# Delta rule block inverses: a second, transposed table in DRAM in place of on-chip transposes

## The chip, the cores and the metric

One Trainium2 chip (trn2), one core. The metric is the device time of one execution in microseconds (us). The kernel before takes 1786.38 us, the median of three runs (1785.5 to 1786.52).

## What is computed

The reference is one inference step of a hybrid decoder layer for 1024 prompt tokens and 8 sampled tokens. The part that the change touches is the gated delta rule of the prompt tokens, four heads of width 128. Cut to what matters:

```python
k = ...; beta = ...; g = cumsum(log decay)          # per head, per chunk
a_mat = where(strict, einsum('cd,sd->cs', k * beta, k) * decay, 0)
sol   = triangular_solve(eye + a_mat, rhs, lower=True)
# scan over chunks: v_new = u - w S;  o = q S + qk v_new;  S = S * decay + k^T v_new
```

The kernel does not solve the triangular system. It forms the inverse of the unit triangular matrix of each chunk of 128 tokens and each head and multiplies by it.

## The kernel before

The program is a single stream for five engines, written with a tile framework that plans the order of the instructions on each engine by a simulated timeline, and fills waits of one part with instructions of others. So the order on an engine is not the order in the code: projections, the top-k search, the query/key normalisation and the scan of the delta rule are interleaved. Within an engine the order is fixed once planned, and an instruction that waits holds up everything behind it on that engine. All DMAs of this part are issued by SyncE (SP), whose queue is in order too.

The parts around the change, in the order of the code:

- `w2`: for each of four heads, projections (`u_tile`), and `dl_local`, which stores the triangular matrices' 32 by 32 diagonal blocks into the DRAM table `d_b` and the whole blocks into `d_Bt`.
- `block_inverse`: loads all 128 diagonal blocks (4 block positions, 8 chunks, 4 heads), one block in each partition, 1024 numbers long, as `B`; inverts them at once by 31 steps of two VectorE instructions (L678 and L680) into `U`; stores `U` to the DRAM table `d_u` (L681). `B` and `U` are two of the four buffers of the tag "c", which `u_tile` uses too.
- `scan`: `dl_setup` clears `Ub` and `Bo` (two buffers each) and then `dl_chunk` runs for eight chunks. It loads six tiles (L1132), calls `dl_inverse`, and makes the chunk's output and the state for the next chunk.
- `dl_inverse(n)`: loads the four diagonal blocks of each head into `Ub` (L1089, four DMAs of 16 KB each), off-diagonal parts into `Bo` (L1092) and `Btl` (L1094); transposes `Ub` for the four heads on TensorE (L1097) into PSUM, tag `pi` with two buffers; copies that to `T0` on ScalarE (L1099); multiplies `Bo` by `T0` (L1102), copies the product to `P1` (L1104), multiplies by `Ub` (L1107) and subtracts (L1109). A second, smaller level follows (L1112 to L1123).
- The projections that fill the waits are the matmuls L163 to L165 with ScalarE evacuating their PSUM banks (L862 for the gates, L692 for queries and keys; two banks); the top-k search counts on ScalarE (L765) and VectorE (L768) in turn; `load_kv` (L993 to L1003) loads keys into the single buffer `kvn`, four small DMAs a round, and transposes them.

What shows as tile `T` in a row of the profile is `T0` or `T1`, since buffer numbers are left out there.

Of the kernel before, what the change touches and what calls it, by code (L numbers as in the profile page):

```python
# [9 lines left out]
F32 = mybir.dt.float32  # L10
# [4 lines left out]
AF = mybir.ActivationFunctionType  # L15
# [39 lines left out]
class K:  # L55
# [368 lines left out]
    def dram(self):  # L424
        dp = self.dp
        self.d_g = dp.tile([16, 128, T], F32, name="d_g")
        self.d_z = dp.tile([4, 128, T], F32, name="d_z")
        self.d_qT = dp.tile([4, 128, 1024], F32, name="d_qT")
        self.d_kT = dp.tile([4, 128, 1024], F32, name="d_kT")
        self.d_kn = dp.tile([1024, 512], F32, name="d_kn")  # L430
        self.d_vn = dp.tile([1024, 512], F32, name="d_vn")
        self.d_qk = dp.tile([128, 8, 4, 128], F32, name="d_qk")
        self.d_D = dp.tile([128, 8, 4, 128], F32, name="d_D")
        self.d_G = dp.tile([32, 128], F32, name="d_G")
        self.d_Bt = dp.tile([128, 8, 4, 128], F32, name="d_Bt")
        self.d_b = dp.tile([4, 8, 4, 32, 32], F32, name="d_b")
        self.d_u = dp.tile([4, 8, 4, 32, 32], F32, name="d_u")
        self.d_q = dp.tile([T, 512], F32, name="d_q")
        self.d_k = dp.tile([T, 128], F32, name="d_k")
        self.d_v = dp.tile([T, 128], F32, name="d_v")  # L440
        self.d_s = dp.tile([8, 6, 128], F32, name="d_s")
        self.d_y = dp.tile([8, 128, T], F32, name="d_y")
        self.d_ob = dp.tile([4, 128, T], F32, name="d_ob")
        self.d_x2 = dp.tile([8, 128, T], F32, name="d_x2")
        self.d_act = dp.tile([22, 128, T], F32, name="d_act")
        self.d_oa = dp.tile([8, 64, 1024], F32, name="d_oa")
# [218 lines left out]
    def block_inverse(self):  # L665

        nc, wk = self.nc, self.wk
        B = wk.tile([128, T], F32, name="c", tag="c", bufs=4)[:, 0:1024].rearrange("p (i c) -> p i c", c=32)
        U = wk.tile([128, T], F32, name="c", tag="c", bufs=4)[:, 0:1024].rearrange("p (i c) -> p i c", c=32)
        nc.sync.dma_start(B.rearrange("p i c -> p (i c)"), self.d_b.rearrange("b n h i c -> (b n h) (i c)"))  # L670
        nc.gpsimd.memset(U, 1.0)
        nc.gpsimd.affine_select(U, U, pattern=[[-1, 32], [1, 32]], compare_op=ALU.is_equal, fill=0.0, base=0,
                                channel_multiplier=0)
        t = self.scratch[:, 1600:1856]
        for j in range(31, 0, -1):
            w = 32 - j
            tv = t[:, :j * w].rearrange("p (a b) -> p a b", a=j)
            nc.vector.tensor_tensor(tv, B[:, 0:j, j:j + 1].to_broadcast([128, j, w]),  # L678
                                    U[:, j:j + 1, j:32].to_broadcast([128, j, w]), op=ALU.mult)
            nc.vector.tensor_tensor(U[:, 0:j, j:32], U[:, 0:j, j:32], tv, op=ALU.subtract)  # L680
        nc.sync.dma_start(self.d_u.rearrange("b n h i c -> (b n h) (i c)"), U.rearrange("p i c -> p (i c)"))  # L681

    def qkv(self, m):

# [384 lines left out]
    def dl_setup(self):  # L1069
        nc, wk, cp = self.nc, self.wk, self.cp  # L1070
        self.dn = cp.tile([128, 1], F32, name="dn")
        nc.sync.dma_start(self.dn, self.I['delta_norm'].rearrange("a c -> c a"))
        self.Ub, self.Bo = [], []
        for j in range(2):
            u = self.up.tile([128, 4, 128], F32, name=f"Ub{j}", bufs=1)
            b = self.up.tile([128, 4, 128], F32, name=f"Bo{j}", bufs=1)
            nc.gpsimd.memset(u, 0.0)
            nc.gpsimd.memset(b, 0.0)
            self.Ub.append(u)
            self.Bo.append(b)  # L1080
        self.St = None

    def dl_inverse(self, n):

        nc, wk = self.nc, self.wk
        Ub, Bo = self.Ub[n % 2], self.Bo[n % 2]
        for b in range(4):
            s = slice(32 * b, 32 * b + 32)
            nc.sync.dma_start(Ub[s, :, s], self.d_u[b, n].rearrange("h i c -> i h c"))  # L1089
        for b in (0, 2):  # L1090
            s, d = slice(32 * b, 32 * b + 32), slice(32 * b + 32, 32 * b + 64)
            nc.sync.dma_start(Bo[s, :, d], self.d_Bt[s, n, :, d])  # L1092
        Bt = wk.tile([64, 4, 64], F32, name="Btl", tag="Btl", bufs=1)
        nc.sync.dma_start(Bt, self.d_Bt[0:64, n, :, 64:128])  # L1094
        p = self.pd("pi")
        for h in range(4):
            nc.tensor.transpose(p[:, h], Ub[:, h], self.ident)  # L1097
        T0 = wk.tile([128, 4, 128], F32, name="T0", tag="T0", bufs=1)
        nc.scalar.activation(T0, p, AF.Copy)  # L1099
        p = self.pd("pi")  # L1100
        for h in range(4):
            nc.tensor.matmul(p[:, h], Bo[:, h], T0[:, h], start=True, stop=True)  # L1102
        P1 = wk.tile([128, 4, 128], F32, name="P1", tag="P1", bufs=1)
        nc.scalar.activation(P1, p, AF.Copy)  # L1104
        p = self.pd("pi")
        for h in range(4):
            nc.tensor.matmul(p[:, h], P1[:, h], Ub[:, h], start=True, stop=True)  # L1107
        U = wk.tile([128, 4, 128], F32, name="U1", tag="U1", bufs=2)
        nc.vector.tensor_tensor(U, Ub, p, op=ALU.subtract)  # L1109
        p = self.pd("pi")  # L1110
        for h in range(4):
            nc.tensor.transpose(p[:64, h, 0:64], U[0:64, h, 0:64], self.ident[:64, :64])  # L1112
        T1 = wk.tile([64, 4, 64], F32, name="T1", tag="T1", bufs=1)
        nc.scalar.activation(T1, p[:64, :, 0:64], AF.Copy)
        p = self.pd("pi")
        for h in range(4):
            nc.tensor.matmul(p[:64, h, 0:64], Bt[:, h, :], T1[:, h], start=True, stop=True)
        P2 = wk.tile([128, 4, 64], F32, name="P2", tag="P2", bufs=1)
        nc.vector.tensor_copy(P2[64:128], p[:64, :, 0:64])
        p = self.pd("pi")  # L1120
        for h in range(4):
            nc.tensor.matmul(p[:64, h, 0:64], P2[64:128, h], U[64:128, h, 64:128], start=True, stop=True)
        nc.scalar.activation(U[0:64, :, 64:128], p[:64, :, 0:64], AF.Copy, scale=-1.0)  # L1123
        return U
# [711 lines left out]
```

## Time and profile before

| | us |
|---|---|
| median of three runs | 1786.38 |
| the profiled execution | 1784.55 |
| its span, first to last instruction | 1782.70 |
| TensorE (PE) busy | 1736.5 |
| VectorE (DVE) busy | 1207.6 |
| ScalarE (ACT) busy | 852.3 |
| GpSimd (POOL) busy | 42.6 |

The profiled execution lies 1.83 us (0.1%) under the median; 1.85 us of it lie outside the span. Times in rows are microseconds from the span's start. Starts and durations of matmuls overlap their neighbours, because they are pipelined; what one costs in a run is the distance of its end from the end before it.

### The profile page before, as it was taken

Reading aid. Unit: us, or ns where it says so; the run is one execution under the profiler, and the core shown is the slowest. Engines: PE = TensorE matmul, PEld = TensorE weight load, DVE = VectorE, ACT = ScalarE, POOL = GpSimd, SP = SyncE. Lnnn points to the kernel's source line nnn. Section 1 sums busy time; section 2 is a strip of 40 time slices with the busy share of each in tenths; the row PEclk is TensorE's granted clock in tenths of the full one; section 3 lists DMA queues with packets and bytes.
Section 4 is the critical chain, followed back from the end, with each engine's and each line's share of the span. In section 5 each row is a group of like instructions: output and inputs, shape, how many; then the busy total and the mean of one; then the engine's idle time right before and its main releaser. Section 6 shows DMA issues by size and latency. Waiting matters only on the chain.

```text
span 1782.7 us, 31712 instructions
## 1 busy us (share of the span) xinstructions
PE 1736.5 (97%) x12276; PEld 1662.9 (93%) x12276; DVE 1207.6 (68%) x2776; ACT 852.3 (48%) x1575; POOL 42.6 (2%) x68
## 2 busy tenths in 40 slices
PE   5999999999999999999999999999999999999999
PEld 5998989999999988878889999999999999999998
DVE  7775658999898867797757488776666665734222
ACT  4568467777834436587634244443333333412012
POOL 3001100000000000010000000000000000000000
PEclk9999999999999999999999999999999999999999
DMA  6114434433645542254568444332222223722122
GB/s 196 40 34 143 138 106 138 145 92 116 176 128 156 170 143 89 84 190 138 173 215 265 135 133 144 96 115 82 84 72 82 85 78 121 229 85 80 46 80 69
DMA packets 293594, 218.00 MB, mean 122 GB/s; under 512 B 39292, under 2 KB 267456, under 8 KB 292412
## 3 DMA queue, kind: packets, MB, share of 16 engines
q1 hardware_dynamic: 291716, 205.50, 38.1%
q0 software_dynamic: 1728, 10.49, 1.7%
q8 instruction: 96, 1.57, 0.4%
q14 instruction: 54, 0.44, 0.1%
HBM read 154.17 MB, written 61.87 MB: 121 GB/s over the span
## 4 chain that ended last, share of the span: by engine, by line
PE 84%; DMA 5%; DVE 5%; issue 3%; ACT 2%; SPq 0%; POOL 0%; ACTq 0%; DVEq 0%; POOLq 0%
PE pj L163 15%; PE pj L165 15%; PE pj L164 15%; PE F L1708 2%; PE F L1710 2%; PE F L1709 2%; PE A L1708 2%; PE A L1709 2%; PE A L1710 2%; PE D L1708 2%; PE D L1710 2%; PE D L1709 2%; PE PT L1055 1%; PE B L1709 1%; PE B L1708 1%
## 5 line engine op out<-in xcount | busy, mean ns | idle before, releaser
L163 PE MATMUL pj<-xhi,whi 128*128 128x344 f32 x912 | 298.6, 327 | 5.3 <-ACT gs L862 4.3
L165 PE MATMUL pj<-xhi,wlo 128*128 128x344 f32 x912 | 295.4, 324 | 0.0
L164 PE MATMUL pj<-xlo,whi 128*128 128x344 f32 x912 | 294.2, 323 | 0.0
L187 ACT ACTIVATE whi<-wraw 128x1024 fp32r<-128x1024 f32 (+4 forms) x126 | 115.3, 915 | 249.3 <-PE pj L164 208.7
L163 PEld LDWEIGHTS pj<-xhi,whi 128*128 128x128 f32 x912 | 172.8, 189 | 9.4 <-ACT gs L862 5.8
L164 PEld LDWEIGHTS pj<-xlo,whi 128*128 128x128 f32 x912 | 172.8, 189 | 2.0 <-issue 1.1
L165 PEld LDWEIGHTS pj<-xhi,wlo 128*128 128x128 f32 x912 | 172.7, 189 | 1.5
L164 PE MATMUL pj<-act,whi 128*128 128x344 f32 x528 | 170.2, 322 | 0.0
L163 PE MATMUL pj<-act,whi 128*128 128x344 f32 x528 | 169.8, 322 | 0.0
L165 PE MATMUL pj<-act,wlo 128*128 128x344 f32 x528 | 168.8, 320 | 0.3 <-DVE wlo L188 0.3
L188 DVE TENSOR_TENSOR wlo<-wraw,whi 128x1024 fp32r<-128x1024 f32 (+3 forms) x104 | 116.4, 1119 | 48.8 <-ACT whi L187 46.7
L1772 DVE TENSOR_TENSOR x<-pj,x 128x344 f32<-128x344 f32 x96 | 48.6, 514 | 141.6 <-PE pj L165 141.4
L768 DVE TENSOR_SCALAR_CACHE_REDUCE kvb<-S,cand 128x384 bf16<-128x384 f32 (+3 forms) x128 | 103.7, 810 | 2.0
L165 PEld LDWEIGHTS pj<-act,wlo 128*128 128x128 f32 x528 | 99.3, 188 | 0.5 <-DVE wlo L188 0.5
L163 PEld LDWEIGHTS pj<-act,whi 128*128 128x128 f32 x528 | 99.3, 188 | 0.5
L164 PEld LDWEIGHTS pj<-act,whi 128*128 128x128 f32 x528 | 99.3, 188 | 0.0
L1709 PE MATMUL A<-hb,wlo 128*128 128x258 f32 x328 | 92.6, 283 | 0.0
L1708 PE MATMUL A<-hb,wlo 128*128 128x258 f32 x328 | 92.5, 282 | 0.0
L1710 PE MATMUL A<-hb,wlo 128*128 128x258 f32 x328 | 92.3, 282 | 0.0
L1708 PE MATMUL D<-hb,wx 128*128 128x258 f32 x308 | 87.1, 283 | 0.0
L1709 PE MATMUL D<-hb,wx 128*128 128x258 f32 x308 | 87.0, 282 | 0.0
L1710 PE MATMUL D<-hb,wx 128*128 128x258 f32 x308 | 87.0, 283 | 0.0
(595 smaller groups left out, 4803.0 us busy)
## 6 DMA issues: line engine op xcount, KB each, us to landing
wraw<-in_w_gate_up SPq DMA_DIRECT2D x50, 512.0 KB
wraw<-in_w_in SPq DMA_DIRECT2D x38, 512.0 KB
d_act<-x SPq DMA_DIRECT2D x41, 258.0 KB
araw<-d_act SPq DMA_DIRECT2D x20, 516.0 KB
d_g<-gs SPq DMA_DIRECT2D x48, 172.0 KB
wraw<-in_w_out SPq DMA_DIRECT2D x16, 512.0 KB
wraw<-in_w_branch SPq DMA_DIRECT2D x12, 512.0 KB
wraw<-in_w_down SPq DMA_DIRECT2D x16, 384.0 KB
```

The costliest lines, as they stand in the source:

```text
L163: nc.tensor.matmul(ps, lh, rh, start=(j == 0), stop=False)
L164: nc.tensor.matmul(ps, lh, rl, start=False, stop=False)
L165: nc.tensor.matmul(ps, ll, rh, start=False, stop=(j == last))
L187: self.nc.scalar.activation(hi, src, AF.Copy)
L188: self.nc.vector.tensor_tensor(lo, src, hi.bitcast(F32), op=ALU.subtract)
L768: nc.vector.tensor_scalar(junk[:r, :n], s, thr[:r, j:j + 1], 0.0, op0=ALU.is_lt, op1=ALU.add, accum_out=cnt[:r, j:j + 1])
L1055: nc.tensor.transpose(p[:, j, :], P[j][:, 128 * s:128 * s + 128], self.ident)
L1708: nc.tensor.matmul(p, lh, rh, start=(first and k == 0), stop=False, skip_group_check=True)
L1709: nc.tensor.matmul(p, lh, rl, start=False, stop=False, skip_group_check=True)
L1710: nc.tensor.matmul(p, ll, rh, start=False, stop=(k == 3), skip_group_check=True)
L1772: nc.vector.tensor_tensor(xv, p, xv, op=ALU.add)
```

## The change

`block_inverse` writes the inverted blocks a second time: a ScalarE copy (Copy activation) reads `U` with rows and columns of each block exchanged and writes over `B`, which is then stored to a new DRAM table `d_ut`. `dl_inverse` no longer transposes: it loads `T0` from `d_ut` by four DMAs a chunk, ahead of those of `Ub`. `T0` has one buffer for all eight chunks, and its off-diagonal parts are cleared once in `dl_setup`. Eight times four transposes and eight ScalarE copies go; one ScalarE copy, one store of 512 KB, 32 loads of 16 KB and one clearing come.

```diff
         self.d_b = dp.tile([4, 8, 4, 32, 32], F32, name="d_b")
+        self.d_ut = dp.tile([4, 8, 4, 32, 32], F32, name="d_ut")
         self.d_u = dp.tile([4, 8, 4, 32, 32], F32, name="d_u")
...
         nc.sync.dma_start(self.d_u.rearrange("b n h i c -> (b n h) (i c)"), U.rearrange("p i c -> p (i c)"))
+        nc.scalar.activation(B, U.rearrange("p i c -> p c i"), AF.Copy)
+        nc.sync.dma_start(self.d_ut.rearrange("b n h i c -> (b n h) (i c)"), B.rearrange("p i c -> p (i c)"))
...
+        self.T0 = self.up.tile([128, 4, 128], F32, name="T0", bufs=1)
+        nc.gpsimd.memset(self.T0, 0.0)
         self.St = None
...
-        Ub, Bo = self.Ub[n % 2], self.Bo[n % 2]
+        Ub, Bo, T0 = self.Ub[n % 2], self.Bo[n % 2], self.T0
         for b in range(4):
             s = slice(32 * b, 32 * b + 32)
+            nc.sync.dma_start(T0[s, :, s], self.d_ut[b, n].rearrange("h i c -> i h c"))
             nc.sync.dma_start(Ub[s, :, s], self.d_u[b, n].rearrange("h i c -> i h c"))
...
-        p = self.pd("pi")
-        for h in range(4):
-            nc.tensor.transpose(p[:, h], Ub[:, h], self.ident)
-        T0 = wk.tile([128, 4, 128], F32, name="T0", tag="T0", bufs=1)
-        nc.scalar.activation(T0, p, AF.Copy)
         p = self.pd("pi")
         for h in range(4):
             nc.tensor.matmul(p[:, h], Bo[:, h], T0[:, h], start=True, stop=True)
```

## Rows read from the trace of the kernel before

**Rows 1.** The page: busy time of each engine; chain that ended last, by engine.
```profile
PE 1736.5 (97%) x12276; PEld 1662.9 (93%) x12276; DVE 1207.6 (68%) x2776; ACT 852.3 (48%) x1575; POOL 42.6 (2%) x68
...
PE 84%; DMA 5%; DVE 5%; issue 3%; ACT 2%; SPq 0%; POOL 0%; ACTq 0%; DVEq 0%; POOLq 0%
```

**Rows 2.** Stages around the change: stretch, length, busy time, PEclk, DMA share, GB/s.
```profile
345.00:440.00 95.00, 95.00 (x631) 94.82 (x630) 88.25 (x256) 72.91 (x127) 2.62 (x7) 1.00 0.38 110
440.00:560.00 120.00, 117.46 (x836) 113.01 (x836) 109.19 (x289) 70.52 (x156) 0.00 (x0) 0.99 0.53 151
560.00:640.00 80.00, 76.18 (x575) 71.14 (x575) 62.50 (x206) 36.11 (x92) 0.00 (x0) 0.98 0.55 155
```

**Rows 3.** Groups by line, 440 to 640: busy us, mean ns, idle before.
```profile
L1097 PE MATMUL pi<-ident,Ub 128*128 128x128 f32 x32 | 5.2, 285 | 0.0
...
L1099 ACT ACTIVATE T<-pi 128x512 f32<-128x512 f32 x8 | 4.7, 591 | 1.1 <-PE pi L1097 1.1
```

**Rows 4.** Timeline of PE, chunk 0: start, duration, instruction.
```profile
451.95 0.32 PE L165 MATMUL pj<-xhi,wlo 128*128 128x344 f32 x1
452.11 0.60 PE L1097 MATMUL pi<-ident,Ub 128*128 128x128 f32 x4
452.46 0.40 PE L163 MATMUL pj<-xhi,whi 128*128 128x344 f32 x1
```

**Rows 5.** Chain in order of time: start, what it adds to the chain, what.
```profile
445.38 5.40 DMA zs<-d_z
...
469.66 0.35 PE pj L165
...
474.86 0.59 PE pi L1097 x4
...
479.77 0.89 PE pi L1102 x8
```

**Rows 6.** ScalarE's instructions of 1024 and of 512 columns, by shape and by line.
```profile
L187 ACT ACTIVATE whi<-wraw 128x1024 fp32r<-128x1024 f32 x72 | 76.1, 1057 | 94.1 <-PE pj L164 71.6 <-issue 9.5 <-PE F L164 5.4
...
L1288 ACT ACTIVATE Ss<-tp x2: 1019/1021/1023, 246.3 to 248.1; 8x512 f32<-8x512 f32 x2
```

**Rows 7.** Timeline of DVE: the last step of the block inverses.
```profile
439.59 0.18 DVE L680 TENSOR_TENSOR c<-c,kvb 128x31 f32<-128x31 f32 x1
```

**Rows 8.** Timeline of ACT just after it.
```profile
439.58 1.03 ACT L765 ACTIVATE kvb<-S,cand 128x896 bf16<-128x896 f32 x1
...
442.42 0.77 ACT L862 ACTIVATE gs<-pj 128x344 f32<-128x344 f32 x2
```

**Rows 9.** Timeline of PE at two stalls; in brackets idle time and its releaser.
```profile
440.79 0.27 PE L701 MATMUL tq<-ident,st 128*8 128x128 f32 x1
442.90 0.43 PE L163 MATMUL pj<-xhi,whi 128*128 128x344 f32 x1 [1.84 <-ACT gs L862]
...
565.93 0.41 PE L997 MATMUL tq<-ident,kvn 128*128 128x128 f32 x2 [0.30 <-DMA kvn<-d_k]
```

**Rows 10.** Stretches: busy times, granted clock, DMA share, GB/s.
```profile
443.60:447.10 3.50, 3.50 (x15) 3.50 (x14) 2.77 (x14) 2.76 (x5) 0.00 (x0) 0.51 0.84 232
...
445.00:450.00 5.00, 5.00 (x27) 5.00 (x27) 4.67 (x14) 3.72 (x9) 0.00 (x0) 0.79 0.91 270
...
455.00:460.00 5.00, 4.30 (x32) 4.11 (x31) 3.97 (x10) 4.61 (x13) 0.00 (x0) 1.00 1.01 306
```

**Rows 11.** Timeline of SP's DMA issues: start, time on the queue, DMA, count.
```profile
439.80 0.34 SPq L681 DMA_DIRECT2D d_u<-c  x1
...
445.82 1.98 SPq L1089 DMA_DIRECT2D Ub<-d_u  x4
...
480.70 1.00 SPq L1092 DMA_DIRECT2D Bo<-d_Bt  x2
...
560.80 3.35 SPq L993 DMA_DIRECT2D kvn<-d_k  x4
```

**Rows 12.** The matmuls that read T0: min/median/max ns, first and last start.
```profile
L1102 PE MATMUL pi<-T,Bo x64: 272/275/421, 456.3 to 613.1; 128*128 128x128 f32 x64
```

## The prediction

> **What bounds the kernel now.** I read the page first: TensorE is busy for 97% of the span and makes up 84% of the chain that ended last [rows 1]. Then the stages that the change touches, by stretches: while the block inverses run on VectorE (up to 440) TensorE has no idle time at all, in the first part of the scan (440 to 560) it lacks 2.5 us, in the second (560 to 640) 3.8 us [rows 2]. So no chain of the delta rule sets the time; TensorE's own work does, plus a few stalls. The scan's waits are filled with projections that have to be done anyway. What the change saves counts as far as it is TensorE time or one of those stalls; a shorter latency of a chunk's inverse counts for nothing. What it adds on ScalarE, SP or the DMA engines counts only where TensorE already waits for these.
>
> **What goes: 32 transposes.** They stand in the groups with 285 ns each [rows 3], but that is a duration, and matmuls overlap. What four of them cost is read from ends. In chunk 0 the projection matmul ahead of them ends at 451.95 + 0.32 = 452.27, the one behind at 452.46 + 0.40 = 452.86; two such in a row end 0.16 us apart (half of their 0.32), so the four cost 0.59 - 0.16 = 0.43 us [rows 4]. In chunk 1 they follow other fp32 matmuls; the chain gives them 0.59 us, but a projection matmul right behind such a run costs 0.35 us in place of 0.16, and would do so with the transposes gone, so 0.59 - 0.19 = 0.40 us [rows 5]. Eight chunks: 3.2 to 3.4 us, and I take 3.3 us. All of it lies on the path while TensorE is full.
>
> The Trainium skill, "TensorE: Matmul & The Clock Gate", Part 4, gives a transpose about 275 ns in a kernel and says that the access latency dominates it. Charged 32 times that would be 8.8 us. This trace has the same duration, but shows it overlapped when four stand in a row; what the page's number would make of the time is a rival below.
>
> **What goes: eight copies of T0 on ScalarE,** 591 ns each, 4.7 us in all, and 1.1 us in which ScalarE stood waiting for the transposes [rows 3]. ScalarE is not the bound (59% busy from 440 to 560 [rows 2]), so I count nothing; the bounds are 0 and the share of ScalarE stalls of TensorE that this could loosen, which is weighed in the first rival.
>
> **What comes: one ScalarE copy of 1024 columns, read transposed.** A contiguous one of that length takes 1.06 us. The only ScalarE instruction in the trace that steps over 16 numbers between neighbours is L1288: 1.02 us for 512 columns [rows 6], where a contiguous one of 512 takes 0.59 [rows 3]. By these, a column costs 0.91 ns contiguous with 0.12 us fixed ((1057 - 591)/512), and 1.75 ns strided; 1024 strided columns make 1.9 us. Bounds 1.06 and 1.9, and I take 1.9, since the copy reads with a stride of 32 numbers. Where does it fall? It can start when the last step of the inverses ends, at 439.77 [rows 7]. That is just where ScalarE is late already: it counts for the top-k search from 439.58 and gets to the evacuation of two projection banks only at 442.42 [rows 8]; TensorE, out of banks, is idle for 1.84 us up to 442.90 [rows 9], and after it runs at half clock (the lower level, 1.2 GHz) from 443.6 to 447.1 [rows 10]. The copy is early in the code and ready then, so I put it ahead of the evacuation: the stall grows by the whole 1.9 us. Bounds: 0 (the evacuation goes first) and 1.9. No second loss for the clock, which has fallen there already.
>
> **What comes: the store of d_ut,** 512 KB behind d_u, at about 442.6, and the loads of T0 behind it. It falls into the busiest DMA stretch, with shares of 0.91 to 1.01 and about 270 to 306 GB/s [rows 10]: 512 KB and the 64 KB of the first T0 take 2.1 us there. Behind it on SP stand the first chunk's loads. In the kernel before, the matmuls L1102 start at 456.3 [rows 12], and T0 is wanted then. Store issued at 442.6, landed after as long as zs needed in this stretch, 5.4 us [rows 5]: 448.0; four T0 issues at the rate of Ub's, 1.98 us [rows 11]; landed 5.4 us later: 455.4. That is just early enough, and the removed transposes and copy are the cover. I count 0; the price without this cover is the slower rival.
>
> **What comes: 32 issues on SP,** four a chunk at 1.98 us [rows 11], 16 us of queue time in all. T0 has one buffer, so its load for chunk n+1 waits until the matmuls L1102 of chunk n are done. What is held up behind that wait? Nothing new: SP already waits for the same event to load Bo; L1102 of chunk 1 ends at 479.77 + 0.89 = 480.66 [rows 5] and Bo's loads go at 480.70 [rows 11]. From there to the next use of T0, one chunk later, there are some 16 to 28 us. The extra 2 us of queue time are free after most chunks, except after chunk 4: there SP is occupied without a gap by the four key loads, for 3.35 us from 560.80 [rows 11], and TensorE then has an idle 0.30 us on them [rows 9]. T0's issues go ahead of these, so the keys come up to 2.0 us later. Bounds 0 (the plan puts T0 behind them) and 2.0; I take the middle, 1.0, since TensorE has other work between its two key transposes. The DMA engines have the room outside the first 20 us, with a share of 0.53 to 0.55 over the two parts of the scan [rows 2]. The clearing of T0 on GpSimd (2% busy [rows 1]) costs nothing.
>
> **Sum.** -3.3 + 1.9 + 1.0 = -0.4 us. I set it against the median: 1786.38 - 0.4 = **1786.0 us**; the profiled execution would go from 1784.55 to 1784.2.
>
> **The rivals.**
> *The stall at 441 goes.* The order is planned anew, and two banks and a count may fall differently; with a few ScalarE copies fewer the evacuation comes in time. Then the 1.84 us idle and the half clock (3.5 us at 0.51, so 1.7 us) are won as well: -3.3 - 1.84 - 1.7 = -6.8, and with the key loads' 1.0 the time is 1780.6. For it: the copies removed. Against it: the new copy stands at that very place.
> *A transpose costs its duration.* 32 x 0.275 us, the median that matmuls of this size show [rows 12], is 8.8 us; 1786.38 - 8.8 + 2.9 = 1780.5. The overlapped ends [rows 4] speak against it. It is the reading that the Trainium skill, "TensorE: Matmul & The Clock Gate", Part 4, suggests.
> *The first chunk waits for the second table* (slower). The chain copy, store, four loads has 0.5 us to spare by the sum above, and takes none of the 2.1 us into account that its own bytes need in a full stretch. If they are additional, T0 lands at 457.5, and Ub, queued behind it by 1.98 us, lands after L1107 wants it. It decides from a landing later than 456. With 3 us idle on TensorE and 1.7 us at half clock after it: 1786.0 + 4.7 = 1790.7. For it: DMA shares near 1 exactly there. Against it: projections that could be moved in.
> *The gain doesn't arrive.* TensorE is held by the evacuations in the scan, and what the transposes free is idle time afterwards: 1786.38 + 2.9 = 1789.3.
>
> **How the numbers follow.** A measurement of this kernel can tell about 0.2% (3.6 us) from no change. Forecast: 0.43 (no change, 1783 to 1789). Stall gone: 0.23, duration counted: 0.04 (both faster). First chunk late: 0.25 (slower). Gain lost: 0.05 (no change). That is faster 0.27, same 0.48, slower 0.25. The range reaches to both outer cases with the unknown costs of each (1.0 us for the keys): 1779.5 to 1791.5.
>
> **What would show it.** In the profile after: no L1097; TensorE's busy time smaller by some 3 us in the scan; one ScalarE copy of 128 x 1024 near 440 with 1.1 to 1.9 us and the evacuation behind it; the idle time ahead of L163 near 441 grown to about 3.7 us; T0's loads next to those of Bo, and no idle time of TensorE whose releaser is a DMA of T0 or Ub. I am wrong if the stall at 441 is gone or elsewhere, if L1102 of chunk 0 waits for a DMA, or if stalls in stages that the change doesn't touch differ by more than 2 us.

## The result, and the profile after

The changed kernel takes 1800.42 us, the median of six runs (1798.48 to 1801.42); the kernel before takes 1785.03 us on the same chip, the median of six runs. The ratio is 1.0076, 95% interval 1.0059 to 1.0093: **slower by 0.76%**, some 13.5 us (the two medians lie 15.4 us apart, inside that interval), where 1786.0 with a range of 1779.5 to 1791.5 was forecast.

| | before, us | after, us |
|---|---|---|
| span of the profiled execution | 1782.7 | 1799.5 |
| TensorE busy | 1736.5 | 1736.6 |
| VectorE busy | 1207.6 | 1208.5 |
| ScalarE busy | 852.3 | 850.8 |

TensorE is as long busy with 32 transposes fewer. In the scan more of its time runs at half clock, but over the whole span the mean granted clock is 0.993 in both executions, so the clock alone doesn't explain it. The stages around the change, after (columns as in [rows 2], which these lines answer to):

```profile
345.00:440.00 95.00, 95.00 (x629) 94.82 (x628) 88.98 (x251) 73.34 (x126) 4.46 (x9) 1.00 0.38 111
440.00:560.00 120.00, 110.70 (x781) 105.84 (x780) 106.94 (x289) 69.52 (x154) 0.00 (x0) 0.96 0.55 154
560.00:640.00 80.00, 72.66 (x525) 68.51 (x524) 61.70 (x196) 33.36 (x82) 0.00 (x0) 0.96 0.52 143
```

Up to 440 TensorE is as full as before. From 440 to 640 TensorE's idle time was 2.5 + 3.8 us [rows 2] and is now 9.3 + 7.3 us, so 10.3 more. Busy time times the missing part of the clock (PEclk) was 117.46 x 0.01 + 76.18 x 0.02 = 2.7 us and is 110.70 x 0.04 + 72.66 x 0.04 = 7.3 us, so 4.6 more. Together that is 14.9 us, where the spans differ by 16.8: most of the loss lies in the scan.

What TensorE waited for from 440 to 660, after (engine, line, releaser: us in total, times, longest):

```profile
PE pj L163 <- ACT gs L865: 7.1, 5, 3.7
PE pi L1118 <- ACT T L1115: 3.2, 2, 2.2
PE pd L1162 <- DVE V L1159: 2.3, 1, 2.3
PE tq L1000 <- DMA kvn<-d_k: 1.5, 1, 1.5
```

The same view of before:

```profile
PE pj L163 <- ACT gs L862: 4.3, 5, 1.8
```

Lines behind the added ones are 1 to 6 higher after. The wait for the new table itself is 0.3 us. What has grown are the waits for the projections' banks (L163, 4.3 to 7.1 us), those for ScalarE and VectorE in the delta rule's own chain (L1118 and L1162, which weren't in the view of before) and the one for the keys `kvn` (0.3 to 1.5 us). One place was forecast closely: the transposed copy on ScalarE takes 1.95 us and stands ahead of the evacuation of two projection banks, and TensorE's stall there, 1.84 us in [rows 9] and forecast at about 3.7, is 3.68. ScalarE, then TensorE, after (start, duration, instruction, in brackets the idle time before it and what ended it):

```profile
442.59 1.95 ACT L683 ACTIVATE c<-c 128x1024 f32<-128x1024 f32 x1
...
445.73 0.77 ACT L865 ACTIVATE gs<-pj 128x344 f32<-128x344 f32 x2
```

```profile
446.21 0.66 PE L163 MATMUL pj<-xhi,whi 128*128 128x344 f32 x1 [3.68 <-ACT gs L865]
```

The order of instructions is the same as before on each engine up to the end of the block inverses, and from there another one on TensorE, VectorE, ScalarE and SP. In the inverse of chunk 0 this is seen at once. Before, projections stand between its steps (460 to 469):

```profile
458.07 1.16 PE L1107 MATMUL pi<-Ub,P 128*128 128x128 f32 x8 [0.70 <-ACT P L1104]
...
468.99 0.68 PE L1117 MATMUL pi<-T,Btl 64*64 64x64 f32 x8
```

After, the steps stand one behind the other, and TensorE waits ahead of each:

```profile
455.83 1.13 PE L1103 MATMUL pi<-T,Bo 128*128 128x128 f32 x8 [0.30 <-DMA T<-d_ut]
...
457.64 1.16 PE L1108 MATMUL pi<-Ub,P 128*128 128x128 f32 x8 [0.69 <-ACT P L1105]
459.64 0.41 PE L1113 MATMUL pi<-ident,U 64*64 64x64 f32 x4 [0.84 <-DVE U L1110]
...
462.23 0.68 PE L1118 MATMUL pi<-T,Btl 64*64 64x64 f32 x8 [2.18 <-ACT T L1115]
```

### The profile page after: what moved, and what is told of

It is laid out like the page before. It is cut to its first block, busy times and chain, and to the rows that moved or that the text cites. A ratio compares the mean times of both kernels' runs of the same rounds, so it can differ in the third digit from the quotient of the medians.

```text
span 1799.5 us, 31692 instructions
## 1 busy us (share of the span) xinstructions
PE 1736.6 (97%) x12244; PEld 1662.9 (92%) x12244; DVE 1208.5 (67%) x2776; ACT 850.8 (47%) x1568; POOL 42.7 (2%) x69
## 4 chain that ended last, share of the span: by engine, by line
PE 56%; DMA 4%; DVE 2%; issue 1%; ACT 1%; SPq 0%; ACTq 0%; DVEq 0%
PE pj L163 8%; PE pj L165 8%; PE pj L164 8%; PE F L1709 2%; PE F L1711 2%; PE F L1710 2%; PE A L1709 2%; PE A L1710 2%; PE A L1711 2%; PE D L1709 2%; PE D L1711 2%; PE D L1710 2%; PE PT L1058 1%; DMA gt<-d_g 1%; PE B L1710 1%
## 5 line engine op out<-in xcount | busy, mean ns | idle before, releaser
L163 PE MATMUL pj<-xhi,whi 128*128 128x344 f32 x912 | 298.1, 327 | 7.8 <-ACT gs L865 7.1
L163 PEld LDWEIGHTS pj<-xhi,whi 128*128 128x128 f32 x912 | 172.7, 189 | 11.7 <-ACT gs L865 8.9
L163 PE MATMUL pj<-act,whi 128*128 128x344 f32 x528 | 169.9, 322 | 0.5 <-ACT whi L187 0.5
L163 PEld LDWEIGHTS pj<-act,whi 128*128 128x128 f32 x528 | 99.3, 188 | 1.3 <-ACT whi L187 0.8
```

The source lines that it names most:

```text
L163: nc.tensor.matmul(ps, lh, rh, start=(j == 0), stop=False)
```

## The experiments

Three theories, A to C in the expectations. *Order* (A): the new order costs the time, whatever was added. *Instructions* (B): what was added costs it, each at its place; a sharper form found on the way is that SP's in-order queue does (S). *ScalarE* (C): the transposes' time on TensorE is waited away again, since ScalarE's queue sets the pace there. To tell order from instructions, "in the order of before" below means that each instruction of an engine is tied to the next one of that engine in the order of the kernel before, by dependencies that need no semaphore (several kernels tied in this way come out within 0.2% of the kernel before, so the ties cost nothing that shows here); "own order" means the planner's. Where T0's loads come along in the order of before, those of chunk 0 stand ahead of Ub's and the later ones behind Bo's. Times of one kernel spread over up to 17 us, so ratios to the kernel before, taken beside it on the same chip, carry the comparisons.

### The parts of the change, in the order of before

**The whole change.**

> The changed kernel with every engine's order held to that of the kernel before (ordering edges without waits); what the change adds stands where that leaves room: the ScalarE copy ahead of the late evacuation as in the changed kernel, the store of d_ut behind that of d_u, T0's loads behind those of Bo. Theory A, the new plan of the whole scan costs the time and not the new instructions: my sum of -0.4 us holds here, 1783 to 1788. Theory B, the copy, the 32 loads and the wait for the single T0 cost the time wherever they stand: 1795 to 1800.

Measured: 1799.97 us, ratio 1.0058 (1.0032 to 1.0084). The new order isn't needed for most of the loss; but this alone doesn't say that the order is innocent.

**The transposes alone left out.**

```diff
-        p = self.pd("pi")
-        for h in range(4):
-            nc.tensor.transpose(p[:, h], Ub[:, h], self.ident)
-        T0 = wk.tile([128, 4, 128], F32, name="T0", tag="T0", bufs=1)
-        nc.scalar.activation(T0, p, AF.Copy)
+        T0 = Ub
```

> The kernel before without the transposes and the copies of T0, in the order of before; the first product reads Ub untransposed, so the transposition is left out of the computation. The gain alone: by my sum -3.3 us against before (both theories), and -8.8 if a transpose costs its full duration. If TensorE only waits elsewhere in its place, 0.

Measured: 1789.90 us, ratio 1.0012 (0.9989 to 1.0034). The forecast 3.3 us do not arrive, though nothing at all is added. TensorE:

```profile
455.49 1.05 PE L1098 MATMUL pi<-Ub,Bo 128*128 128x128 f32 x8
...
458.86 1.58 PE L1103 MATMUL pi<-Ub,P 128*128 128x128 f32 x8 [2.31 <-ACT P L1100]
```

and ScalarE:

```profile
454.86 1.28 ACT L1141 ACTIVATE kn<-kn,kdec 128x128 f32<-128x128 f32 x4 [1.00 <-DMA kn<-d_kn]
...
458.23 0.57 ACT L1100 ACTIVATE P<-pi 128x512 f32<-128x512 f32 x1
```

TensorE comes to the second product after a wait of 2.31 us where it was 0.70 before. P1's copy stands on ScalarE behind the scalings of chunk 1's kn and vn and a top-k count, and these wait for kn's DMA. In the kernel before the copy T0 stands in that place, and the scaling behind it doesn't wait:

```profile
453.44 0.57 ACT L1099 ACTIVATE T<-pi 128x512 f32<-128x512 f32 x1
454.06 1.28 ACT L1145 ACTIVATE kn<-kn,kdec 128x128 f32<-128x128 f32 x4
```

So the copy that left ScalarE had only filled a wait.

**The copy and the store alone**, transposes kept, nobody reads the new table.

```diff
+        nc.scalar.activation(B, U.rearrange("p i c -> p c i"), AF.Copy)
+        nc.sync.dma_start(self.d_ut.rearrange("b n h i c -> (b n h) (i c)"), B.rearrange("p i c -> p (i c)"))
```

> The kernel before with the transposes kept, plus only the transposed ScalarE copy (128 x 1024) and the store of 512 KB to the second table, which nobody reads; every engine's order is that of before, with the copy where the changed kernel has it. Theory A: the stall ahead of the projection banks near 441 grows by 1.9 us to 3.7 and nothing else follows: 1.9 us, up to 3 with half clock behind it, so 1790 to 1791. Theory B (copy and store are the price of the changed kernel in the old order): 8 to 11 us, 1796 to 1799, part of it at half clock. If it is 0, the copy's stall is given back later.

Measured: 1787.97 us, ratio 1.0013 (0.9990 to 1.0037). The stall near 441 is 3.7 us here too; its 1.9 us are within the interval, and the some 10 us that the whole change cost in this order are above it.

**The loads alone**: no copy, no store, T0 loaded from `d_u`.

```diff
-            nc.sync.dma_start(T0[s, :, s], self.d_ut[b, n].rearrange("h i c -> i h c"))
+            nc.sync.dma_start(T0[s, :, s], self.d_u[b, n].rearrange("h i c -> i h c"))
```

> The changed kernel without the transposed copy and its store: T0 is loaded by the same 32 DMAs into the same single buffer, but from the table of the blocks that are not transposed (so the inverse is not that of the reference); every engine's order is that of before, T0's loads behind those of Bo. Theory A: the loads are free, so the time is that of the kernel with the transposes merely left out in the old order, 0 to 2 us over before: 1788 to 1790. Theory B (loads and SP's waits for the single buffer cost the time): 6 to 10 us over before, with idle time of TensorE whose releaser is a DMA or L1103, or later key loads.

Measured: 1797.04 us, ratio 1.0063 (1.0040 to 1.0085): the loads are the price in this order. SP's queue:

```profile
446.62 1.92 SPq L1091 DMA_DIRECT2D T<-d_u  x4
448.67 3.37 SPq L1092 DMA_DIRECT2D Ub<-d_u  x4
...
453.96 0.50 SPq L1130 DMA_DIRECT2D kn<-d_kn  x1
```

SP's queue where the transposes are left out and nothing is loaded:

```profile
446.92 1.92 SPq L1089 DMA_DIRECT2D Ub<-d_u  x4
...
451.50 0.34 SPq L1128 DMA_DIRECT2D kn<-d_kn  x1
```

With the loads, the load of chunk 1's kn goes 2.5 us later. ScalarE stands waiting for it with P1's copy of chunk 0 behind it:

```profile
458.64 1.28 ACT L1143 ACTIVATE kn<-kn,kdec 128x128 f32<-128x128 f32 x4 [5.03 <-DMA kn<-d_kn]
...
462.02 0.57 ACT L1102 ACTIVATE P<-pi 128x512 f32<-128x512 f32 x1
```

and TensorE behind that:

```profile
462.64 2.08 PE L1105 MATMUL pi<-Ub,P 128*128 128x128 f32 x8 [6.34 <-ACT P L1102]
```

T0 and Ub, the tiles that were asked after in the forecast, are long there; the tile that is late is one that the change doesn't touch.

### The same loads from another queue

**Loads alone, issued by GpSimd.**

```diff
-            nc.sync.dma_start(T0[s, :, s], self.d_u[b, n].rearrange("h i c -> i h c"))
+            nc.gpsimd.dma_start(T0[s, :, s], self.d_u[b, n].rearrange("h i c -> i h c"))
```

> As the run with T0's loads alone in the old order (from the table that is not transposed, so the inverse is not the reference's), but the 32 loads are issued by GpSimd, whose queue has nothing else from 422 to 761 us, so SP's queue is that of the kernel without loads. Same bytes, same buffer, same order elsewhere. Theory S (SP's in-order queue: four more issues ahead of the loads of kn and vn of chunk 1, for which ScalarE waits with P1's copy of chunk 0 behind it): kn of chunk 1 is issued near 451.5 and not 454.0, the wait of TensorE for P1's copy near 455 falls from 6.3 to about 2.3 us, and the time to that of the kernel with the transposes left out in the old order, 1787 to 1791. Rival (the loads' bytes crowd the DMA engines between 444 and 460, and kn lands late whoever issues): the wait stays at 5 to 6 us and the time at 1795 to 1798.

Measured: 1787.36 us, ratio 0.9998 (0.9981 to 1.0015). The loads still move the same bytes, from another engine's queue (and in other packets: 1024 on the DMA queue q0, where SP's loads were 4608 on q1). GpSimd, SP, ScalarE and TensorE at the same place:

```profile
443.19 2.30 POOL L1091 DMA_DIRECT2D T<-d_u  x4 [19.75 <-DMA d_u<-c]
```

```profile
451.24 0.34 SPq L1130 DMA_DIRECT2D kn<-d_kn  x1
```

```profile
455.23 1.28 ACT L1143 ACTIVATE kn<-kn,kdec 128x128 f32<-128x128 f32 x4 [1.29 <-DMA kn<-d_kn]
```

```profile
459.23 1.16 PE L1105 MATMUL pi<-Ub,P 128*128 128x128 f32 x8 [2.17 <-ACT P L1102]
```

kn is issued at 451.24 and not at 453.96, ScalarE waits 1.29 in place of 5.03 us, TensorE 2.17 in place of 6.34. Of the 3.4 us by which ScalarE's scaling of kn starts earlier, 2.7 are the earlier issue; the other 0.7 lie between issue and start, where the packets may have a part. From 440 to 480 the DMA engines carry the same share of 0.67 at 191 GB/s in both kernels (first with SP, then with GpSimd):

```profile
440.00:480.00 40.00, 31.82 (x197) 30.54 (x196) 28.73 (x83) 30.37 (x64) 0.00 (x0) 0.91 0.67 191
```

```profile
440.00:480.00 40.00, 35.99 (x219) 34.52 (x219) 30.23 (x86) 32.68 (x68) 4.47 (x8) 0.91 0.67 191
```

TensorE's wait of 1.1 us for the keys `kvn` behind chunk 4 (at 570.88 with SP's queue) is gone too. So issuing these loads on SP costs the time, and not their bytes; that the order within SP's queue does it is read from the issue times, and T0's loads put behind kn's on SP itself, the direct test, was not run. The Trainium skill, "DMA: Bandwidth & Descriptors", section "Issuing engines are not separate DMA queues", says that issuing from several engines "will only save the time on the sequencer it takes to initiate the DMA, which is usually small relative to the DMA itself". The equal DMA shares (0.67) agree that there is no other gain. That the time is small doesn't hold as a measure here: with what stood behind it, the issuing was worth 0.65% of the kernel (1.0063 against 0.9998), 11.6 us, uncertain by about 5. The two profiled executions differ by 6.8 us, of which the wait for P1's copy is 4.2.

**The whole change, T0's loads issued by GpSimd**, order of before.

> The whole change, order of before on all engines, transposed copy where the changed kernel has it, T0's 32 loads issued by GpSimd and not by SP. Theory S: the change in the old order (1800.0) loses what SP's queue cost, 7 to 9 us; what stays is the 1.9 us of the longer stall near 441 (which came out as 0.3 to 2.3 us when it was alone) and the 1.9 us by which the kernel without transposes in the old order was slower: 1788 to 1793. Rival (store and loads together crowd the DMA engines): 1796 to 1801, with TensorE's wait for P1's copy at 4 us or more.

Measured: 1787.47 us, ratio 0.9995 (0.9974 to 1.0016), where the same with SP's queue was 1.0058. The 1.9 us of the copy's stall (3.68 us here too) are not told apart from 0 in the time.

### The order

**Transposes left out, in the order of the changed kernel.**

> The same work (no transposition, no copy, no second table, no loads of T0), but in the order of the changed kernel. Theory A (the plan): still slow, 9 to 14 us over before, since only the 1.9 us of the copy and some queue time are gone. Theory B (the new instructions): 3 us faster than before, as in the old order.

Measured: 1797.71 us, ratio 1.0045 (1.0026 to 1.0065). There are no loads and no copy in it, only less work, and it is slower by 8 us. What TensorE waited for from 440 to 660:

```profile
PE pj L163 <- ACT gs L862: 4.9, 4, 1.8
PE pi L1113 <- ACT T L1110: 3.4, 1, 3.4
PE pd L1157 <- DVE V L1154: 2.8, 1, 2.8
```

These are the waits of the changed kernel in its inverse (3.2 us there) and state (2.3 us).

**Transposes left out, the planner's own order.**

> The same work again, with the order that the planner makes for it. Theory A: the plan can fall either way, so this may differ from the one in the old order by several us with the same work. Theory B: the same as in the old order within 1.5 us.

Measured: 1796.55 us, ratio 1.0052 (1.0033 to 1.0071): another order, the same loss.

**The kernel before with one column copied.** One column of U is copied by ScalarE, or by GpSimd, into the dead buffer B, which was to make the planner draw up a new order for unchanged work.

```diff
+        nc.scalar.activation(B[:, 0, 0:1], U[:, 0, 0:1], AF.Copy)
```

> The kernel before with all its work, transposes included, plus one ScalarE instruction that copies a single column of U into the dead buffer B behind the last step of the block inverses (some 0.2 us of ScalarE). It is there only because it makes the planner draw up a new order for all that follows. Theory A (what costs time is that the order is drawn up anew behind 440 us, whatever is added or removed): slower by 5 to 12 us, 1793 to 1800, beside the kernel before on this chip at about 1788. Theory B (the added copy, store and loads cost the time, each at its place): within 1 us of the kernel before, since nothing of them is in it. In between (2 to 5 us) would mean that orders scatter by that much and this one is a milder draw.

Measured: 1788.19 us, ratio 1.0005 (0.9983 to 1.0027).

> As the run with the ScalarE column, but the single column is copied by GpSimd, so no engine of the stage has any work more: a second draw of the planner on unchanged work. Theory A: slower by 5 to 12 us, not necessarily as much as the other draw. Theory B: within 1 us of the kernel before. If one draw is slower by over 5 us and the other is not, an order's price is luck and no property of re-planning.

Measured: 1788.05 us, ratio 1.0008 (0.9986 to 1.0031). The premise was wrong: the planner left the order as it was, with GpSimd's column entirely, with ScalarE's but for a few instructions. So the two say nothing on orders; they show that these comparisons return 1 within 0.1% when nothing changes. The same column copied by VectorE does change the order (2,686 of TensorE's 11,772 instructions stand elsewhere):

> The kernel before with all its work and one column copied by VectorE into the dead buffer B behind the last step of the block inverses (under 0.2 us). Of the kernels with one such column it is the one whose order is drawn up anew over the whole scan (2,686 of TensorE's instructions stand elsewhere). Theory: any newly drawn order loses, because the order of before is a lucky one: slower by 5 to 15 us. Rival: only orders drawn up without the transposes lose: within 3 us of the kernel before.

Measured: 1782.88 us, ratio **0.9971** (0.9951 to 0.9990): faster than the kernel before, by nothing but another order.

**The copy and the store, transposes kept, own order.**

> The kernel before with the transposes kept, plus the transposed ScalarE copy and the store of the second table that nobody reads, in the order that the planner draws up for it (2,597 of TensorE's instructions stand elsewhere). The same work in the order of before had a ratio of 1.0013 to the kernel before. Theory that any newly drawn order loses: 1.004 to 1.011, 1794 to 1807. Rival, only orders without the transposes lose: 0.999 to 1.003, 1785 to 1792.

Measured: 1802.65 us, ratio 1.0074 (1.0046 to 1.0102), where the order of before gave the same instructions 1.0013. So both theories of that pair fall: a new order doesn't always lose, and it doesn't lose only without the transposes. Orders scatter.

Where the good and the bad order part is seen in the stage at the start of the scan. The column copied by VectorE, stretch 440 to 560, and the products of chunk 0's inverse on TensorE:

```profile
440.00:560.00 120.00, 119.03 (x859) 114.57 (x858) 110.22 (x289) 71.42 (x158) 0.00 (x0) 1.00 0.56 154
```

```profile
457.93 1.05 PE L1103 MATMUL pi<-T,Bo 128*128 128x128 f32 x8
464.34 1.05 PE L1108 MATMUL pi<-Ub,P 128*128 128x128 f32 x8
```

The same of the table's kernel in its own order:

```profile
440.00:560.00 120.00, 110.70 (x775) 106.33 (x774) 102.06 (x276) 69.71 (x152) 0.00 (x0) 0.96 0.52 146
```

```profile
456.08 1.13 PE L1105 MATMUL pi<-T,Bo 128*128 128x128 f32 x8
460.84 2.08 PE L1110 MATMUL pi<-Ub,P 128*128 128x128 f32 x8 [3.63 <-ACT P L1107]
```

In the fast order 6.4 us lie between the starts of the first and the second product, filled with projections, and TensorE waits for none of them; it is idle 1.0 us in 120. In the slow one 4.8 us lie between these starts, 3.63 of these are a wait, and it is idle 9.3 us and partly at half clock. The changed kernel stands with the latter, also with 9.3 us. In both of these 3.7 us are the stall near 441 behind the copy.

**The changed kernel with T0's loads issued by GpSimd, own order.**

> The changed kernel with one word changed: T0's loads are issued by GpSimd instead of SP; the planner's own order, drawn up anew. Theory S alone (SP's queue is the whole price): 1788 to 1793. With the price of an order in which the inverse of chunk 0 stands without filler on TensorE (the kernel without transposes and without loads took 1796.6 in its own order): 1796 to 1800, so most of the loss stays, and there are then two causes, each of 7 to 10 us, that do not add up.

Measured: 1809.32 us, ratio 1.0111 (1.0087 to 1.0135), against 0.9995 for the same instructions in the order of before: some 21 us by order alone, the largest difference of this kind, and more than either forecast had.

**The changed kernel's own order, T0's loads issued by GpSimd.**

> The changed kernel, every engine in the changed kernel's own order, only T0's 32 loads issued by GpSimd and no longer by SP. If SP's queue is the price there too: 1787 to 1792. If the order is the whole price: 1797 to 1802, as the changed kernel and as the kernel without transposes in this order (1797.7). If both count: 1793 to 1797.

Measured: 1796.91 us, ratio 1.0050 (1.0033 to 1.0067). With it the two causes stand in a square (ratios to the kernel before):

| | T0 by SP's queue | T0 by GpSimd's queue |
|---|---|---|
| order of before | 1.0058 | 0.9995 |
| order of the changed kernel | 1.0076 | 1.0050 |

Counted from 0.9995, either alone costs some 0.55 to 0.63%, both together 0.81%. They do not add up. In the changed kernel's order SP's queue is worth 0.26% (4.6 us); the intervals of these two just overlap, so that size is uncertain. TensorE's wait of 1.5 us for `kvn` and the second wait of 1.1 us for T1's copy (L1118), both there in the changed kernel, are gone. The latter is the same chain as above, at chunk 2: in the changed kernel SP issues its kn at 476.77, ScalarE waits for it, and T1's copy of chunk 1 stands behind:

```profile
480.99 1.28 ACT L1146 ACTIVATE kn<-kn,kdec 128x128 f32<-128x128 f32 x4 [2.07 <-DMA kn<-d_kn]
```

```profile
485.84 0.68 PE L1118 MATMUL pi<-T,Btl 64*64 64x64 f32 x8 [1.06 <-ACT T L1115]
```

With GpSimd's queue kn is issued at 473.62, and ScalarE waits 0.64 us.

**Where the order loses.** The order of before up to the end of the inverse of chunk 1 (near 490 us), then the planner's order of the kernel with 1809.32; and the reverse.

> The changed kernel with T0's loads on GpSimd's queue. Instructions stand in the order of before up to the end of the inverse of chunk 1 (near 490 us) and behind that in the order which the planner drew up for this kernel (1809.3 in its own order all through, 1787.5 in the order of before all through). If such an order loses at the start of the scan, where the first chunk's inverse stands on TensorE without filler: 1788 to 1794. If it loses in the later chunks and at the end of the scan (580 to 660): 1799 to 1809.

> The reverse: the planner's own order up to the end of the inverse of chunk 1, and behind that what is left in the order of before. If the loss is at the start: 1797 to 1809. If it is in the later chunks: 1788 to 1796. If both halves come out near 1798, the loss is spread over the whole scan.

Measured: 1810.79 us, ratio 1.0118 (1.0097 to 1.0139), and 1802.34 us, ratio 1.0071 (1.0044 to 1.0097). So the planner's order loses in both parts. In the first kernel the start is that of the good order, and then TensorE waits from 480 to 555, where before it doesn't wait at all:

```profile
PE pd L1162 <- DVE V L1159: 4.4, 1, 4.4
```

The two losses, 0.0123 and 0.0076 over 0.9995, make more than the whole order's 0.0116; a seam between two orders may cost something of its own, and what each half costs is not known closer than this.

### What ScalarE holds back

**P1's copy of chunk 0 moved ahead** of the scaling of vn and a count, in the whole change with GpSimd's queue and the order of before.

> As the run before it, with one ScalarE instruction moved: P1's copy of chunk 0 stands between the scalings of kn and vn of chunk 1 and not behind vn's scaling and a top-k count. Theory C (what the transposes free on TensorE is waited away again, since the copy P1 comes no earlier on ScalarE's in-order queue): the wait for P1's copy near 456 falls from about 2.3 to under 1 us, and the time by 1 to 2 us beside the run before it: 1786 to 1791. If theory C is wrong the wait moves to the next instruction (the projection banks) and the time is the same as the run before it.

Measured: 1790.25 us, ratio 1.0014 (0.9994 to 1.0034), against 0.9995 (0.9974 to 1.0016) without the move. TensorE without the move, then with it:

```profile
460.93 1.16 PE L1108 MATMUL pi<-Ub,P 128*128 128x128 f32 x8 [1.98 <-ACT P L1105]
```

```profile
460.09 1.16 PE L1108 MATMUL pi<-Ub,P 128*128 128x128 f32 x8 [0.69 <-ACT P L1105]
...
462.61 0.43 PE L163 MATMUL pj<-xhi,whi 128*128 128x344 f32 x1 [1.37 <-ACT gs L865]
...
467.75 0.42 PE L163 MATMUL pj<-xhi,whi 128*128 128x344 f32 x1 [0.77 <-ACT gs L865]
```

The wait for P1 falls from 1.98 to 0.69 us as expected, and 1.37 and 0.77 us come behind it, ahead of the projections whose banks ScalarE now evacuates later. The time doesn't fall, so theory C doesn't hold for P1's copy alone: as its counter-forecast said, the wait moves to the next instruction.

**The transposed copy moved behind the evacuation near 441.**

> As the change in the order of before with T0's loads on GpSimd's queue (1787.5), but the transposed ScalarE copy stands behind the evacuation of the two projection banks near 441 and no longer ahead of it. If the copy only delays what stands behind it on ScalarE, the stall ahead of the projections goes back from 3.7 to 1.8 us: 1785 to 1788. If the copy's 1.9 us are waited away elsewhere (ScalarE's wait for kn behind it has 1.1 us of room), the time stays: 1787 to 1789. A first T0 that comes too late (its store goes 1 to 2 us later) would give 1789 to 1792 and a wait of TensorE for T near 456.

Measured: 1790.66 us, ratio 1.0015 (0.9997 to 1.0033). TensorE:

```profile
443.93 0.56 PE L163 MATMUL pj<-xhi,whi 128*128 128x344 f32 x1 [1.84 <-ACT gs L865]
454.93 0.42 PE L163 MATMUL pj<-xhi,whi 128*128 128x344 f32 x1 [1.64 <-ACT gs L865]
...
462.99 1.16 PE L1108 MATMUL pi<-Ub,P 128*128 128x128 f32 x8 [3.13 <-ACT P L1105]
```

The stall near 441 goes back to 1.84 us, and the waits behind it grow: 1.84 + 1.64 + 3.13 = 6.6 us, against 3.68 + 1.98 = 5.7 with the copy in front. So moving one ScalarE instruction out of TensorE's way made TensorE wait at the next one, both times. In these traces TensorE's saved time is waited for, from 441 to 465, on ScalarE's queue, which itself waits for kn's loads. None of these versions of the change is faster than the kernel before; the one kernel that is, is the kernel before with a column copied by VectorE (0.9971).

## Why the prediction was wrong

**"So no chain of the delta rule sets the time; TensorE's own work does."** This is the step from which the rest followed, and it failed. TensorE was 95 to 98% busy in the scan [rows 2], in an order in which ScalarE's and VectorE's results came just in time. Full is not the same as alone: with 3.3 us less to do it waited 2.31 us, in place of 0.70, at the first place where ScalarE came no earlier.

**-3.3 us for the transposes.** No gain arrived: ratio 1.0012 (0.9989 to 1.0034) with the transposes left out in the order of before. The work itself did shrink by about that. An estimate from the profiles: TensorE's busy time, less its part lost to the clock (busy time times the missing clock, in stretches of 10 us), is 1727.5 us on average in the four kernels in the order of before that keep the transposes (the two with a column copied by ScalarE or GpSimd counted in), and 1724.4 in the five without transposes and without T0's loads on SP. TensorE's idle time is 48.9 and 52.9 us in the same two groups. So it had some 3 us less to do and 4 us more to wait; single profiles lie within some 4 us of these means. The rival "the gain doesn't arrive" had this, with a chance of 0.05 and another engine step in mind (evacuations alone).

**"I count nothing" for the eight copies of T0.** Right in size, but the reason given, that ScalarE is not the bound, isn't the one that was seen: in chunk 0 the copy had filled a wait for kn, and TensorE does wait for ScalarE there.

**+1.9 us for the transposed copy.** Duration (1.95 us) and stall (3.68 us) came as worked out. For the duration some luck was in it: L1288, from which the price per column was taken, steps over 16 numbers where it writes, and the copy steps over 32 where it reads. In the time it is 0.13%, not told apart from 0 (interval to 0.37%), and the wait moves elsewhere when the copy does.

**0 for the store and the first loads; "nothing new" held up on SP.** This is the first of the two steps that made the result. I followed the new tile to its use, and the tile behind it (Ub) to its use, and both were nearly in time: TensorE waited 0.3 us for T0. (By its own rows the sum left 456.3 - 455.4 = 0.9 us to spare for T0, not the 0.5 that the rival names; nothing hangs on it.) I did not follow what else stood behind four issues on SP: in the order of before chunk 1's kn, 2.5 us later, for which ScalarE waits with P1's copy behind it; in the changed kernel chunk 2's kn, with T1's copy behind it. The price in the order of before is 11 us (1.0058 against 0.9995), give or take 6, and in the changed kernel's order 4.6 us, give or take 4. The rival "the first chunk waits for the second table" had the right engine, time and sign, 4.7 us, and the wrong tile.

**+1.0 us for the key loads.** The wait on them was 0.30 us [rows 9] and is 1.5 us, 1.2 more, and it is gone with GpSimd's queue in the same order. In the order of before it came where it was forecast, behind chunk 4 (1.1 us); in the changed kernel the late keys are a round behind those that follow T0's issues. Size and queue were right.

**The order.** "The order is planned anew" stood in the text, as a chance for a gain at one stall. As a cost it had no term, and that is the second step. The same instructions, in the order of before and in the planner's own (ratios to the kernel before):

| | order of before | own order |
|---|---|---|
| before, a column copied by VectorE | (that of before: 1) | 0.9971 |
| transposes left out | 1.0012 | 1.0052 |
| copy and store added | 1.0013 | 1.0074 |
| the change, T0 by GpSimd's queue | 0.9995 | 1.0111 |
| the change, T0 by SP's queue | 1.0058 | 1.0076 |

The order alone is worth -0.3 to +1.2% here; the largest of these is several times what the change itself could save (0.2%). A forecast from the terms of the edit, each right, would have needed a range of that width. At the start of the scan the slow orders show as steps of chunk 0's inverse that stand close together with waits ahead of them, in the changed kernel and in the table's own order; a good start can be followed by losses later. That is read from profiles and was not tried by moving these steps alone, and why the planner leaves them room in one case and not in another stays open.

**What would show it** held in part: the forecast named a wait of chunk 0's L1102 for a DMA as a sign of error, and it is there (0.3 us). The larger new waits, at L1118 and L1162, stand in the scan itself and were named by no sign.

## What to carry to other kernels

When a change adds issues to an in-order queue, follow every transfer behind them to the engine that waits for it, and what waits behind that engine; a load that is in time for its own use can still make another late. A queue that is empty in that stretch is worth trying: one word here was worth 0.6% in the order of before. It must be judged in the same order too: with the order that the planner drew up around it, the changed kernel with the same word came out at 1.0111, where it was 1.0076. And where a planner draws up the order, time an edit also in the old order: here new orders of nearly the same work ran from 0.3% faster to 1.1% slower, and an edit worth 0.2% can't be judged by one draw.

## What the runs showed of the hardware

The ScalarE copy that reads with a stride of 32 numbers takes 1.95 us for 1024 columns; the estimate from L1288, which writes with a stride of 16, was 1.9.

TensorE's clock fell with hardly any idle time just ahead of it. In the whole change in the order of before TensorE is busy for 5.95 of the 6.00 us from 655 to 661, the granted clock is 1.00 there, and the last work before the fall was 16 matmuls of two columns each:

```profile
659.59 1.95 PE L1466 MATMUL tq<-skq,st 128*128 128x2 f32 x16
```

```profile
664.00:684.00 20.00, 20.00 (x77) 18.46 (x76) 9.81 (x35) 7.86 (x12) 0.00 (x0) 0.50 0.39 115
```

From 664 to 684 it runs at 0.50, the lower level (1.2 GHz), fully busy: 10 us lost. In the profile of before such a group of 16 stands at 651.50, and the clock over 640 to 700 is 1.00. The fall is not the change's either: in the kernel before with one column copied by ScalarE, nearly the same order, the group stands at 648.69, and behind it is

```profile
655.00:658.00 3.00, 3.00 (x9) 2.32 (x8) 2.16 (x6) 0.77 (x1) 0.00 (x0) 0.50 0.52 157
```

So the group doesn't always bring the fall; no run here takes it away, and the cause stays open.

Part of what the slow kernels lose is clock and not waits. The mean granted clock over all runs of a kernel is 0.9892 for the whole change in the order of before, 0.9922 for the same with GpSimd's queue, and 0.9848 for the latter in the planner's own order (the kernel before: 0.994 beside each). An estimate, these differences times some 1740 us of busy time, gives 5 of the 11 us between the first two and 13 of the 21 us between the last two. Between the two orders of the kernel without transposes (both 0.991) it is under 1 of 6 us. Why the clock is lower in some of them was not tried.
